# Three score blocks in flight, and the second range's norm ahead of the rotary work, in a two-layer hybrid decoder on one core

## The chip, the core and the metric

The kernel runs on one core of a Trainium2 chip. The core has five engines, each of which takes its own instructions strictly in a fixed order: TensorE (PE, matmuls, with its weight loads listed as PEld), VectorE (DVE), ScalarE (ACT), GpSimd (POOL) and SyncE (SP, which only issues DMAs here). The metric is the device time of one execution in microseconds (us). The kernel before took 1122.07 us, the median of three runs (1121.68 to 1123.77).

## What is computed

A sequence of 16 learned meta tokens and 512 tokens, width 1024, passes two layers. Cut to what matters:

```
a = rmsnorm(h, mix_pre_g);  proj = a @ w_in          # q 512, k 128, v 128, b, c, hc 512 each
q, k = partial_rope(q), partial_rope(k)              # 16 of 64 dimensions are rotated
s = q k^T / 8, causal, window 128, in blocks of 128 queries x 256 keys
m = max(max(s), sink);  e = exp(s - m)
p = e / (sum(e) + exp(sink - m));  y_attn = p @ v
y_conv = b * depthwise_conv3(c * hc)
y = concat(rmsnorm(y_attn), rmsnorm(y_conv)) @ w_out;  h += rmsnorm(y, mix_post_g)
f = relu(rmsnorm(h) @ w_up)^2;  h += rmsnorm(f @ w_down, mlp_post_g)
```

All of it is float32.

## The kernel before

**Tiles.** Activations lie transposed, features on the 128 partitions and tokens along the free dimension, in two token ranges: RA (0 to 272, in layer 1 mostly 16 to 272) and RB (272 to 528). A float32 product is made of two parts for each operand (`a_hi`, `a_lo`, `f_hi`, `f_lo`, `whi`, `wlo`) and three matmuls for each of eight k-steps (`mm3`, traced as L192, L193, L194). A tile of 128 outputs on one range is thus 24 matmuls of 128x256 or 128x272. Weights arrive through SP's queue (L162) and are split by ACT (L107) and DVE (L108).

**Stages.** Each layer runs `first_tiles`, `mixer`, an output projection and a `boundary`; then `first_tiles` again for the MLP's first tiles, `mlp` and a `boundary`. At a boundary `Post` adds the normed result to h for one range: its `start` makes the norm's factor, and `steps(i)` runs two k-steps, each of a multiply (L320 or L322) and an add into h (L323) on DVE, a copy to `a_hi` (L329) and a square (L275) on ACT, the rest `a_lo` (L334) and the sum of squares (L276) on DVE. `first_tiles` runs five tiles on RA (K, V and three of the query tiles q0 to q2, or the MLP's first five) while RB's steps (`pB.steps`) run beside them, then three tiles on RB at once, which need every `a_hi` and `a_lo` of RB, then two more. Tiles leave PSUM through evacuations: for K and queries `rope_evac` copies the raw tile (ACT, L549), sends four small DMAs on SP's queue that swap the rotated halves (L554, L555), and leaves for later the rotary arithmetic (DVE L559 to L561) and the split into parts (K: ACT L598, DVE L603; queries: ACT L610, DVE L613). V is scaled (L577) and later transposed by PE (L583). The MLP's tiles are evacuated at L901.

**The mixer.** A list `plan` holds 26 tiles in order: the last query tile q3 on both ranges, then c, h and b tiles of the convolution. A table filled by `put` says what goes between the tiles of the plan. Attention has eight blocks n, each with three steps: S[n] (`scores`: eight matmuls L198, the masks with the maxima on DVE L655, exponentials on ACT L644, then the sums' reciprocals L647 and L648 and the scaling L650 on DVE), T[n] (`transp`: eight PE transposes L690, whose results are split by ACT L279 and DVE L280 into the tile p), and A[n] (`attend`: four matmuls L198 with V, then L703). Layer 0 has a ninth, small block for the meta tokens (`meta_scores`, `meta_transp` L722, `meta_attend`). S[0] and S[1] are put after plan tiles 4 and 5, T[0] after tile 7, and each further T[n] two or three tiles after the one before (`PERIODS`); S[n+2] stands with A[n]. A score tile S takes a buffer of the ring tagged "w", 14 buffers shared with the split weights and the p tiles; its small companions (`mx`, `ng`, `dn`, `se`) have three buffers each. `fast` keeps two of the MLP's operand sums in a tile `tx` of its own.

**Order.** The program text is not the order of the engines: a scheduler works out at build time, from durations that it assumes, in which order the instructions of each engine stand. On the chip that order is fixed, and each instruction waits for its inputs and for a free buffer.

## Time and profile before

| | before |
|---|---|
| time, median of three runs | 1122.07 us |
| the profiled execution | 1120.94 us, of which its span 1119.2 us and 1.74 us around it |
| PE busy | 1079.4 us, 96% of the span |
| DVE busy | 821.4 us, 73% |
| ACT busy | 627.7 us, 56% |
| mean granted PE clock | 0.987 of full speed |

The span is counted from 0. PE is the engine that does nearly all of the work's time, so the first question at any place is where PE is idle and what ends that idle time. PEclk is the granted clock of PE in shares of full speed. A row of the timeline begins with its start and its busy time in us, and ends with the idle time ahead of it and what released it, if there was any; consecutive equal instructions stand in one row with a count. The busy time of one instruction overlaps that of the next, so that what an instruction costs its engine is the distance from its start to the next one's.

### The profile page before, as it was taken

To read this page: it belongs to the slowest core of one execution; us is meant where nothing else is said; L and a number is where in the kernel's file an instruction comes from. 1 tells how busy PE (TensorE), PEld (TensorE's weight loads), DVE (VectorE), ACT (ScalarE), POOL (GpSimd) and SP (SyncE) were. 2 spreads that over 40 slices of the span, in tenths; PEclk is the share of its full clock that TensorE was granted. 3 is DMA by queue.
4 is the path that set the end of the run, shared out by engine and by line. 5 is a ranking of instruction groups with operands and counts; after the bars stand their busy time and mean duration, and the time that the engine had idled before them with its cause. 6 is when DMAs were issued, how large, how long until landed. Compare 5 with 4: busy or idle time off the path is not lost.

```text
span 1119.2 us, 21378 instructions
## 1 busy us (share of the span) xinstructions
PE 1079.4 (96%) x8066; PEld 1035.5 (93%) x8066; DVE 821.4 (73%) x1943; ACT 627.7 (56%) x1510; POOL 11.2 (1%) x46
## 2 busy tenths in 40 slices
PE   9989899999999999999996999999999999999995
PEld 8989899999999999999986989998889989989995
DVE  7988985978486586486588979869946856856835
ACT  8655656665473274275365556666835724724732
POOL 2000000000000000000000000000000000000000
PEclk9999999999999999999998999999999999999998
DMA  8242221342243243134132322222422522522402
GB/s 249 60 121 77 58 76 57 95 133 71 62 126 102 59 125 110 58 112 143 29 102 60 89 67 62 81 76 76 132 79 73 152 75 76 151 76 76 142 1 76
DMA packets 197608, 102.04 MB, mean 91 GB/s; under 512 B 7360, under 2 KB 197456, under 8 KB 197504
## 3 DMA queue, kind: packets, MB, share of 16 engines
q1 hardware_dynamic: 196640, 99.88, 30.7%
q8 instruction: 63, 1.03, 0.4%
q10 hardware_dynamic: 688, 0.58, 0.2%
q14 instruction: 41, 0.34, 0.1%
q0 software_dynamic: 176, 0.21, 0.1%
HBM read 97.88 MB, written 2.10 MB: 89 GB/s over the span
## 4 chain that ended last, share of the span: by engine, by line
PE 83%; DVE 10%; ACT 2%; DMA 2%; issue 1%; SPq 1%; DVEq 0%; ACTq 0%
PE ps L192 26%; PE ps L194 26%; PE ps L193 26%; PE ps L198 2%; DVE wlo L108 2%; PE ps L690 1%; DMA wraw<-in_w_in 1%; DVE a_lo L334 1%; DVE h L323 1%; DVE acc L276 1%; PE ps L231 1%; DMA h<-in_xT 1%; SPq L554 1%; DMA z<-t 0%; DVE S L655 0%
## 5 line engine op out<-in xcount | busy, mean ns | idle before, releaser
L193 PE MATMUL ps<-f_lo,whi 128*128 128x256 f32 (+2 forms) x1072 | 325.8, 306 | 0.0
L194 PE MATMUL ps<-f_hi,wlo 128*128 128x256 f32 (+2 forms) x1072 | 325.6, 305 | 0.0
L192 PE MATMUL ps<-f_hi,whi 128*128 128x256 f32 (+2 forms) x1072 | 323.0, 307 | 0.0
L192 PE MATMUL ps<-a_hi,whi 128*128 128x256 f32 (+3 forms) x808 | 229.5, 297 | 11.1 <-ACT a_hi L329 9.0
L193 PE MATMUL ps<-a_lo,whi 128*128 128x256 f32 (+3 forms) x808 | 233.6, 293 | 3.7 <-DVE a_lo L334 3.5
L194 PE MATMUL ps<-a_hi,wlo 128*128 128x256 f32 (+3 forms) x808 | 231.7, 291 | 0.0
L194 PEld LDWEIGHTS ps<-f_hi,wlo 128*128 128x128 f32 x1072 | 202.3, 189 | 9.1
L193 PEld LDWEIGHTS ps<-f_lo,whi 128*128 128x128 f32 x1072 | 201.7, 188 | 9.5
L108 DVE TENSOR_TENSOR wlo<-wraw,whi 128x512 fp32r<-128x512 f32 x264 | 173.3, 687 | 49.9 <-ACT whi L107 27.5
L192 PEld LDWEIGHTS ps<-f_hi,whi 128*128 128x128 f32 x1072 | 199.6, 188 | 9.4
L107 ACT ACTIVATE whi<-wraw 128x512 fp32r<-128x512 f32 x264 | 153.6, 623 | 88.6 <-PE ps L193 60.8
L192 PEld LDWEIGHTS ps<-a_hi,whi 128*128 128x128 f32 x808 | 150.1, 192 | 15.7 <-ACT a_hi L329 10.4
L193 PEld LDWEIGHTS ps<-a_lo,whi 128*128 128x128 f32 x808 | 154.8, 192 | 8.5 <-DVE a_lo L334 5.5
L194 PEld LDWEIGHTS ps<-a_hi,wlo 128*128 128x128 f32 x808 | 154.8, 192 | 1.9 <-DVE wlo L108 0.2
L506 DVE TENSOR_TENSOR z<-z,ps 128x272 f32<-128x272 f32 (+2 forms) x78 | 38.0, 487 | 100.2 <-PE ps L194 100.1
L193 PE MATMUL ps<-a_lo,wf 128*128 128x264 f32 (+1 forms) x384 | 108.0, 283 | 0.0
L192 PE MATMUL ps<-a_hi,wf 128*128 128x264 f32 (+1 forms) x384 | 107.9, 283 | 0.0
L194 PE MATMUL ps<-a_hi,wf 128*128 128x264 f32 (+1 forms) x384 | 107.2, 283 | 0.0
L107 ACT ACTIVATE wf<-wraw 128x512 fp32r<-128x512 f32 x96 | 59.7, 626 | 84.2 <-PE ps L193 51.4
L107 ACT ACTIVATE wf<-u 128x512 fp32r<-128x512 f32 x72 | 45.2, 628 | 88.0 <-PE ps L193 73.6
L108 DVE TENSOR_TENSOR wf<-wraw,wf 128x512 fp32r<-128x512 f32 x96 | 65.8, 688 | 11.1 <-ACT wf L107 10.1
L193 PEld LDWEIGHTS ps<-a_lo,wf 128*128 128x128 f32 x384 | 72.3, 188 | 0.1
(175 smaller groups left out, 1813.3 us busy)
## 6 DMA issues: line engine op xcount, KB each, us to landing
wraw<-in_w_up SPq DMA_DIRECT2D x128, 256.0 KB
wraw<-in_w_down SPq DMA_DIRECT2D x128, 256.0 KB
wraw<-in_w_in SPq DMA_DIRECT2D x72, 256.0 KB
wraw<-in_w_out SPq DMA_DIRECT2D x32, 128.0 KB
wraw<-in_w_out SPq DMA_DIRECT2D x16, 256.0 KB
h<-in_xT SPq DMA_DIRECT2D x4, 272.0 KB
h<-in_xT SPq DMA_DIRECT2D x4, 256.0 KB
outT<-h SPq DMA_DIRECT2D x8, 128.0 KB
```

The lines of the kernel that those rows point to most:

```text
L107: ACT.activation(hi, raw, AF.Copy)
L108: DVE.tensor_tensor(lo, raw, hi.bitcast(F32), ALU.subtract)
L192: PE.matmul(ps, whi, ahi, start=first, stop=False, skip_group_check=onto)
L193: PE.matmul(ps, whi, alo, start=False, stop=False, skip_group_check=onto)
L194: PE.matmul(ps, wlo, ahi, start=False, stop=last, skip_group_check=onto)
L198: PE.matmul(ps, a[n], b[n], start=first and n == 0, stop=last and n == 1)
L231: PE.matmul(ps, ones[:, which, :], acc, start=True, stop=more is None)
L276: return (eng or DVE).tensor_tensor(acc, acc, sq, ALU.add)
L323: DVE.tensor_tensor(hk, hk, t, ALU.add)
L334: DVE.scalar_tensor_tensor(a_lo[:, k, t0:t1], hk, g, a_hi[:, k, t0:t1].bitcast(F32), ALU.mult, ALU.subtract)
L506: DVE.tensor_tensor(zz, zz, ps, ALU.add)
L554: nc.sync.dma_start(sw[b:b + 8, :], raw[b + 8:b + 16, :])
```

## The change

Three things are changed.

1. Score tiles get a tag "x" of their own with three buffers. Three blocks of scores are issued ahead (S[0] to S[2] after plan tiles 4, 5 and 6; then S[n+3] with A[n]). T[0] moves from after tile 7 to after tile 8, and every further T[n] stands two tiles after the one before, so that T[7] stands after tile 22 where it stood after 23. `mx`, `ng`, `dn` and `se` have four buffers.
2. The tile `tx` is gone; `mlp` takes three tiles of the tag "x" in its place.
3. In `first_tiles` the next steps of RB's norm are called ahead of the evacuations, two of the four calls after the first group of tiles and two after the next one (`initial`, the kernel's start: one after each of the first four).

```diff
-PERIODS = (2, 2, 3, 2, 2, 3, 2, 2)
+PERIODS = (2, 2, 2, 2, 2, 2, 2, 2)
+AHEAD = 3
...
-    tx = cp.tile([P, 3, 4, L // 2], F32R, name="tx")
...
                 evs += mms([iA[i]], act, hooks)
+            for n in (0, 1)[:1 if initial else 2]:
+                m = next(steps, None)
+                if m is not None:
+                    pB.steps(m)
 
             ready = [evs] if initial else [evs[:3]] if i == at[0] else [[ev] for ev in evs]
...
                 evs = [] if initial else evs[3:] if i == at[0] else []
-            for n in (0, 1)[:1 if len(group) == 1 else 2]:
-                m = next(steps, None)
-                if m is not None:
-                    pB.steps(m)
...
-            S = wp.tile([P, 4, 256], F32, tag="w", name="S", bufs=2 * CAP)
-            mxt = tp.tile([P, 4], F32, tag="mx", name="mx", bufs=3)
+            S = wp.tile([P, 4, L // 2], F32, tag="x", name="S", bufs=3)[:, :, :256]
+            mxt = tp.tile([P, 4], F32, tag="mx", name="mx", bufs=4)
...
-        put(at, S[0])
-        put(at + 1, S[1])
+        for n in range(AHEAD):
+            put(at + n, S[n])
...
-        pos = at + 3
+        pos = at + AHEAD + 1
...
-            if n + 2 < 8:
-                put(pos + 1, S[n + 2])
+            if n + AHEAD < 8:
+                put(pos + 1, S[n + AHEAD])
...
-        tv = [view(k_hi), view(k_lo), view(vv.rearrange("p a b c -> p a (b c)"))] + [tx[:, i, :, :n] for i in range(3)]
+        tv = [view(k_hi), view(k_lo), view(vv.rearrange("p a b c -> p a (b c)"))] + [t[:, :, :n] for t in txs[l]]
...
+        txs[l] = [wp.tile([P, 4, L // 2], F32R, tag="x", name="tx", bufs=3) for _ in range(3)]
```

Line numbers below are those of the kernel before; the changed kernel's lines stand one or two further on from the places of the edits.

What the edits do to the order of an engine shows at three places. The first is DVE at the start of layer 1, while PE runs K, V and the queries: the last steps of RB's norm (L322, L323, L334, L276 in turn) among the rotary work of RA. Before, the last 12 rows up to the second to last `a_lo`:

```order
L559 TENSOR_TENSOR t<-z 128x256
L560 TENSOR_TENSOR t<-t,z 128x256
L322 SCALAR_TENSOR_TENSOR t<-z,gt,s 128x256
L613 TENSOR_TENSOR f_hi<-t,f_hi 64x256
L613 TENSOR_TENSOR f_lo<-t,f_lo 64x256
L561 TENSOR_TENSOR t<-t 128x256
L323 TENSOR_TENSOR h<-h,t 128x256
L560 TENSOR_TENSOR t<-t,z 128x256
L322 SCALAR_TENSOR_TENSOR t<-z,gt,s 128x256
L613 TENSOR_TENSOR f_hi<-t,f_hi 64x256
L613 TENSOR_TENSOR f_lo<-t,f_lo 64x256
L334 SCALAR_TENSOR_TENSOR a_lo<-h,gt,a_hi 128x256
```

And after:

```order
L322 SCALAR_TENSOR_TENSOR t<-z,gt,s 128x256
L334 SCALAR_TENSOR_TENSOR a_lo<-h,gt,a_hi 128x256
L323 TENSOR_TENSOR h<-h,t 128x256
L276 TENSOR_TENSOR acc<-acc,t 128x256
L322 SCALAR_TENSOR_TENSOR t<-z,gt,s 128x256
L334 SCALAR_TENSOR_TENSOR a_lo<-h,gt,a_hi 128x256
L323 TENSOR_TENSOR h<-h,t 128x256
L276 TENSOR_TENSOR acc<-acc,t 128x256
L334 SCALAR_TENSOR_TENSOR a_lo<-h,gt,a_hi 128x256
L276 TENSOR_TENSOR acc<-acc,t 128x256
L108 TENSOR_TENSOR wlo<-wraw,whi 128x512 x5
L559 TENSOR_TENSOR t<-z 128x272
```

K's first rotary row, `L559 t<-z 128x272`, stood ten rows ahead of the first of these, and with it the rotary work of K and of two query tiles stood ahead of or among the last two norm steps; now it stands behind them and behind five weight splits.

The second place is DVE in layer 0's mixer, from the scaling of the second score block (S[1], `L650 128x144 x4`) to that of the meta tokens (`L650 s<-s,dn 64x16 x2`). Before:

```order
L650 TENSOR_SCALAR S<-S,dn 128x144 x4
L647 TENSOR_TENSOR dn<-dn,se 64x2
L648 RECIPROCAL dn<-dn 64x2
L650 TENSOR_SCALAR s<-s,dn 64x16 x2
L280 TENSOR_TENSOR p<-ps,p 128x512 x2
```

And after:

```order
L650 TENSOR_SCALAR S<-S,dn 128x144 x4
L647 TENSOR_TENSOR dn<-dn,se 128x4
L648 RECIPROCAL dn<-dn 128x4
L650 TENSOR_SCALAR S<-S,dn 128x256 x4
L647 TENSOR_TENSOR dn<-dn,se 64x2
L757 TENSOR_TENSOR u<-u,ps 128x256
L765 SCALAR_TENSOR_TENSOR z<-u,gt,z 128x272
L280 TENSOR_TENSOR p<-ps,p 128x512
L648 RECIPROCAL dn<-dn 64x2
L280 TENSOR_TENSOR p<-ps,p 128x512
L765 SCALAR_TENSOR_TENSOR z<-u,gt,z 128x272
L108 TENSOR_TENSOR wlo<-wraw,whi 128x512 x2
```

The meta tokens' scaling, the row after the last of these, moved behind the third score block's scaling, behind both splits of the first block's transposes and behind two weight splits.

The third place is PE around the transposes of the meta tokens (L722). Before, they stand directly ahead of the second score block's transposes (`L690 x8`), behind all of A[0] (`p,vv`):

```order
L198 MATMUL ps<-p,vv 128x512
L193 MATMUL ps<-a_lo,whi 128x256
L194 MATMUL ps<-a_hi,wlo 128x256
L192 MATMUL ps<-a_hi,whi 128x256
L193 MATMUL ps<-a_lo,whi 128x256
L194 MATMUL ps<-a_hi,wlo 128x256
L192 MATMUL ps<-a_hi,whi 128x256
L193 MATMUL ps<-a_lo,whi 128x256
L194 MATMUL ps<-a_hi,wlo 128x256
L722 MATMUL ps<-ident,s 128x64 x2
L690 MATMUL ps<-ident,S 128x128 x8
```

And after, from the rest of the first block's transposes (`L690 x6`) on:

```order
L690 MATMUL ps<-ident,S 128x128 x6
L192 MATMUL ps<-a_hi,whi 128x256
L193 MATMUL ps<-a_lo,whi 128x256
L194 MATMUL ps<-a_hi,wlo 128x256
L192 MATMUL ps<-a_hi,whi 128x256
L193 MATMUL ps<-a_lo,whi 128x256
L194 MATMUL ps<-a_hi,wlo 128x256
L722 MATMUL ps<-ident,s 128x64
L198 MATMUL ps<-p,vv 128x512 x4
```

The first of the two transposes of the meta tokens (L722) now stands six matmuls behind the first block's last transposes, ahead of A[0]; before, both stood behind A[0].

## The prediction

> **What bounds the kernel now.** I read the page first, then the busy time by stage, then the timeline of PE at the stages where it is idle, and last the engines that it waits for there.

> The page says that PE is busy nearly throughout:

> ```profile
> span 1119.2 us, 21378 instructions
> PE 1079.4 (96%) x8066; PEld 1035.5 (93%) x8066; DVE 821.4 (73%) x1943; ACT 627.7 (56%) x1510; POOL 11.2 (1%) x46
> ```

> So PE is idle for 1119.2 - 1079.4 = 39.8 us, and since the change leaves the matmuls as they are, it can win only out of these, and out of slow clock behind them. The stages (PE's busy time is the second number; DVE's the fourth):

> ```profile
> 60.00:80.00 20.00, 15.67 (x117) 15.41 (x116) 16.68 (x67) 10.72 (x35) 0.10 (x1) 0.91 0.39 111
> 130.00:140.00 10.00, 6.66 (x44) 6.48 (x44) 8.90 (x33) 4.03 (x13) 0.00 (x0) 0.84 0.29 83
> 215.00:230.00 15.00, 13.54 (x100) 12.16 (x99) 14.16 (x41) 10.26 (x28) 0.00 (x0) 1.00 0.00 1
> 575.00:600.00 25.00, 14.87 (x103) 13.52 (x103) 21.69 (x56) 12.71 (x33) 0.94 (x3) 0.82 0.14 39
> 640.00:660.00 20.00, 17.36 (x141) 16.69 (x139) 15.49 (x54) 11.33 (x32) 0.10 (x1) 1.00 0.19 54
> 775.00:785.00 10.00, 8.40 (x56) 7.02 (x56) 9.16 (x27) 6.60 (x18) 0.00 (x0) 1.00 0.00 0
> ```

> Idle there: 4.3, 3.3, 1.5, 10.1, 2.6 and 1.6 us, 23.4 in all. The rest lies mostly at the start and at the end, which the change leaves alone. The waits themselves, each in brackets with what ended it:

> ```profile
> 71.41 0.41 PE L690 MATMUL ps<-ident,S 128*128 128x128 f32 x2 [4.33 <-DVE S L650]
> 135.45 0.41 PE L690 MATMUL ps<-ident,S 128*128 128x128 f32 x2 [3.34 <-DVE S L650]
> 597.25 1.01 PE L192 MATMUL ps<-a_hi,whi 128*128 128x256 f32 x3 [7.54 <-ACT a_hi L329]
> 651.53 0.44 PE L690 MATMUL ps<-ident,S 128*128 128x128 f32 x2 [1.28 <-DVE S L650]
> 656.83 0.50 PE L198 MATMUL ps<-p,vv 128*128 128x512 f32 x1 [1.35 <-ACT p L279]
> ```

> The first two and the fourth are transposes that wait for a score block's scaling: T[0] and T[6] of layer 0, and a block of layer 1. The third is the start of RB's tiles in layer 1, waiting for the norm. A long wait costs more than itself. In windows of 1 us the last number but two is the granted clock:

> ```profile
> 72.00:73.00 1.00, 1.00 (x7) 1.00 (x6) 0.93 (x4) 1.00 (x8) 0.07 (x1) 0.50 0.00 0
> 75.00:76.00 1.00, 1.00 (x9) 1.00 (x9) 0.00 (x0) 0.16 (x1) 0.00 (x0) 0.80 0.00 0
> 138.00:139.00 1.00, 1.00 (x6) 1.00 (x6) 0.16 (x1) 0.79 (x4) 0.00 (x0) 0.50 0.06 16
> 652.00:653.00 1.00, 1.00 (x11) 1.00 (x10) 1.00 (x4) 0.00 (x0) 0.00 (x0) 1.00 0.00 0
> ```

> After the waits of 4.33 and 3.34 us PE runs at half clock for some 3.3 us (6 or 7 matmuls a us where the full clock gives 8 to 9), a loss of about 1.6 us each, and the stage of the 7.54 us shows a mean clock of 0.82; after the wait of 1.28 us there is none of it.

> **Layer 0's mixer, the middle and the end.** T[6] stood 3.34 us for its scaling. With three blocks ahead, S[6] is issued one T earlier; counting DVE's instructions in the new order, each at its distance of starts in the trace (a mask 0.34 by the two rows below), its scaling is due at about 113, and PE gets to T[6] at about 129. The wait goes, and so does the half clock: 3.34 + 1.6 = 5.0 us gained. DVE's sum for S[7] is 114 against 137 on PE, so nothing of the kind is late next.

> **Layer 0's mixer, the start.** Here a wait takes the place of the one removed. DVE's rows of before (scaling of S[0], scaling for the meta tokens, the first split):

> ```profile
> 70.97 0.90 DVE L650 TENSOR_SCALAR S<-S,dn 128x144 f32<-128x144 f32 x4
> 74.31 0.37 DVE L650 TENSOR_SCALAR s<-s,dn 64x16 f32<-64x16 f32 x2
> 76.47 1.29 DVE L280 TENSOR_TENSOR p<-ps,p 128x512 fp32r<-128x512 f32 x2 [1.80 <-ACT p L279]
> 80.36 0.42 DVE L655 CUSTOM_DVE_ANT_0 S<-ps,mk 128x256 f32<-128x256 f32 x1
> 80.70 0.42 DVE L655 CUSTOM_DVE_ANT_0 S<-ps,mk 128x256 f32<-128x256 f32 x1
> 81.67 0.34 PE L722 MATMUL ps<-ident,s 64*128 64x64 f32 x2
> ```

> T[0] stands one tile and one score block later on PE (2.95 + 0.95 us of cover), so PE reaches it at 71.0 and not at 67.1. S[2]'s four masks (4 x 0.34) now stand ahead of S[0]'s scaling, which moves from 70.97 to about 72.2. T[0] waits about 1.6 us instead of 4.33, too short for the clock. But the meta tokens' scaling stands behind seventeen more rows, and the way from S[0]'s scaling to it is long: two scalings of 128x144 (2 x 0.82), one of 128x256 (1.05, by size from those), two splits (1.22), two weight splits of the same shape (1.22), four convolution steps of 0.4, two of 0.35 and the small rows between them, 8.6 us in all, so that it ends near 80.8. PE reaches the first L722 behind 24 matmuls and eight transposes, 72.7 + 3.7 = 76.4. It waits 4.4 us, and the matmuls of A[0] queue behind it. By then before and after have done nearly the same (before stood at 80.7 with this work), so T[0]'s gain is all given back, and the new half clock costs what the old one did on top, since the old one is in the 80.7: -1.6 us. This wait is worked out from sums of rows; its bounds are no wait at all (+4.3) and one 1.4 us longer (-3.0).

> **The MLP's boundaries.** RB's norm steps go ahead of the evacuations L901 at the two MLP starts, whose waits are the sums of six short ones:

> ```profile
> PE ps L193 <- DVE a_lo L334: 0.7, 3, 0.3
> PE ps L192 <- ACT a_hi L329: 0.7, 3, 0.2
> 227.27 0.49 DVE L334 SCALAR_TENSOR_TENSOR a_lo<-h,gt,a_hi 128x256 fp32r<-128x256 f32 x1 [0.58 <-ACT a_hi L329]
> ```

> The last `a_lo` came at 227.27; by DVE's sum it now comes at 225.35, while PE without waits wants it at 224.7. Of 1.46 us, 0.65 stays: +0.8 here, as much at 775 to 785, +1.5 together. Bounds: 0, where ACT's copies, not DVE, set the pace (half of the waits name them), and 3.1.

> **The start of layer 1.** The last norm steps stood among the rotary work of RA:

> ```profile
> 587.49 0.44 DVE L559 TENSOR_TENSOR t<-z 128x272 f32<-128x272 f32 x1 [0.86 <-DMA z<-t]
> 598.17 0.42 DVE L323 TENSOR_TENSOR h<-h,t 128x256 f32<-128x256 f32 x1
> 599.17 0.48 DVE L334 SCALAR_TENSOR_TENSOR a_lo<-h,gt,a_hi 128x256 fp32r<-128x256 f32 x1 [0.24 <-ACT a_hi L329]
> 601.41 0.60 PE L231 MATMUL ps<-acc,ones 128*128 128x256 f32 x2
> ```

> In the new order the last add into h is due at 589.7 and the last `a_lo` at 590.2, 9.0 us earlier; PE then runs the three tiles at full clock and ends them at 591.0 instead of 601.41, 10.4 us ahead. The rotary work, though, is not gone, it starts later, and its DMAs with it. SP's first and last of RA's 16 and of RB's 24 rotary DMAs, and the weight loads between them:

> ```profile
> 583.30 0.71 SPq L554 DMA_DIRECT2D z<-t  x1
> 594.02 0.62 SPq L555 DMA_DIRECT2D z<-t  x1
> 602.23 2.81 SPq L162 DMA_DIRECT2D wraw<-in_w_in  x5
> 606.46 0.66 SPq L554 DMA_DIRECT2D z<-t  x1
> 622.18 0.62 SPq L555 DMA_DIRECT2D z<-t  x1
> ```

> They go out every 0.7 us (15.72 / 23 and 10.72 / 15). ACT's raw copies (L549) now stand behind the last `a_hi`, so RA's first goes out at about 590.4 and its last at 601.1; after three weight loads (2.81 / 5 each, 1.7) RB's run from 603.7 to 619.4, 2.8 us earlier than before. On DVE, five weight splits (to 594.9) and all of RA's and RB's rotary work follow. DVE is what limits it then:

> ```profile
> 610.00:640.00 30.00, 29.85 (x250) 29.54 (x248) 28.52 (x92) 16.45 (x48) 1.24 (x5) 1.00 0.31 86
> 624.49 0.42 DVE L613 TENSOR_TENSOR f_hi<-t,f_hi 64x256 fp32r<-64x256 f32 x1
> 626.63 0.28 PE L198 MATMUL ps<-k_hi,f_hi 128*128 128x256 f32 x1
> 626.75 0.28 PE L198 MATMUL ps<-k_lo,f_hi 128*128 128x256 f32 x1
> 633.12 0.41 PE L690 MATMUL ps<-ident,S 128*128 128x128 f32 x2
> ```

> The second half of S[1] needs the query tile q3 of RA, whose split stood at 624.49. DVE's rows up to it add up to 619.75 without a single wait; with some waits for DMAs and ACT, as before, it is 622 to 624. PE, now early, reaches that half at 617.1 after a wait of 1.7 us for V's scaling (L583). It waits 3 to 6.5 us there and loses 1.6 us of clock. With S[2] and one tile more behind it than before's T[0] at 633.12, PE reaches T[0] at 635.9 in the worse case, 1.0 us ahead of before after allowing for that work, and 6.6 us ahead with neither idle DVE nor slow clock. I take 623.0: +2.3 of the 10.4 us. That is nearer the worse end, because all sums without idle time are lower bounds. The bounds below: -1.2 if V's wait too lasts over 3 us.

> **The rest of layer 1's mixer.** Scalings are ready five tiles ahead of their transposes, so the waits of 1.28 and 1.35 go: +2.6 (0 to 3.6, with smaller ones at 630 to 700).

> **Sum.** +5.0 - 1.6 + 1.5 + 2.3 + 2.6 = 9.8 us off the profiled execution's 1120.94, thus 1111.1. That execution ran 1.13 us under the median of 1122.07, so the forecast for the median is 1122.07 - 9.8 = 1112.3. The tile tag for `tx` moves no DVE or PE row; the fourth buffers and S's own ring only lift limits.

> **The clock again.** The 1.6 us behind each new wait are read off the rows: the wait of 3.34 us already dropped it. [...]

> **Rivals.**

> *The whole gain arrives* (chance 0.13). The meta tokens' scaling is not late and q3 arrives as DVE's bare sum says: 4.3 + 5.0 + 3.1 + 6.6 + 3.6 = 22.6, 1099.5 us. For it: DVE has idle time in 74 to 78 (the 1.80 above). Against: DVE is in order, and 8.6 us of rows stand ahead of L722's input.

> *New waits, full clock* (0.10). Two waits of over 4 us that do not drop the clock: 2 x 1.6 more, 1109.1. Against it speak all three waits over 3 us above.

> *Rotary work bounds layer 1's start* (no change, 0.07). If RB's DMAs keep their distance from RA's first (606.46 - 583.30 = 23.2), q3 comes 7.1 us later than before, at 633; PE waits 16 us, and that stage stands 7.8 behind: 5.0 - 1.6 + 1.5 - 7.8 + 2.6 = -0.3, about 1122.4.

> *The table is too dense for DVE* (slower, 0.05). Two periods of three tiles became two in each layer. If DVE's work per block, not the distance from S to T, decides, each of the four places waits a tile, 24 x 0.118 = 2.83 us by the two L198 rows above, 11.3 us in all, and T[6]'s 5.0 do not come: 9.8 - 5.0 - 11.3 = -6.5, 1128.6 us. It decides once DVE runs 16 us later at S[6] than its sum of 113; DVE's idle time, 3.3 of 20 us in the stage from 60 to 80 alone, speaks against that.

> **How the numbers follow.** My case has 0.65. A measurement of this kernel can tell 0.2%, 2.2 us, from no change. Faster by more: 0.65 + 0.13 + 0.10, less 0.02 for my own case's loose end: 0.86. Half of those 0.02 goes to same, with the third rival 0.08, and half to slower, 0.06. The range leaves out the last rival and the outer part of the first: 1103 to 1121.

> **What would show it.** Right: no wait at T[6]; one of about 4 us at L722 with half clock behind it, near 76; RB's tiles in layer 1 start by 584 and end near 591; a wait of 3 to 6 us at the L198 of S[1]. Wrong: waits at transposes in mid mixer, RB's tiles held by a PSUM bank that an evacuation has not freed, or no new wait at all.

## The result, and the profile after

The changed kernel takes 1110.99 us, the median of four runs (1109.8 to 1113.09), against 1122.21 us of the kernel before beside it: a ratio of 0.990, 95% interval 0.988 to 0.992, or 11.2 us. The profiled execution took 1113.09 us with a span of 1111.3 us; it is the slowest of the four, with the lowest mean clock (0.985, the others 0.987 to 0.990). On record stood 1112.3. Two runs took far longer than the others of their kernels and are left out of all medians: one of the kernel before (1758.49 us) and one of the kernel with the meta tokens two tiles later (3321.59 us).

The page of after, against 1119.2 us and 1079.4 us of PE:

```profile
span 1111.3 us, 21393 instructions
PE 1079.6 (97%) x8066; PEld 1038.4 (93%) x8066; DVE 819.8 (74%) x1943; ACT 627.0 (56%) x1510; POOL 11.2 (1%) x46
```

PE's work is the same, its idle time fell from 39.8 to 31.7 us. The stages of after, of which the first, third and last were shown of before:

```profile
60.00:80.00 20.00, 16.27 (x123) 15.87 (x121) 18.45 (x79) 14.58 (x49) 0.10 (x1) 0.91 0.43 123
80.00:100.00 20.00, 17.34 (x113) 16.30 (x114) 14.68 (x52) 7.91 (x26) 0.10 (x1) 0.83 0.19 54
575.00:600.00 25.00, 22.01 (x170) 20.53 (x168) 20.90 (x53) 15.18 (x38) 1.04 (x4) 1.00 0.07 18
600.00:640.00 40.00, 35.21 (x257) 34.97 (x258) 36.76 (x121) 25.38 (x73) 0.20 (x2) 0.87 0.35 98
640.00:660.00 20.00, 20.00 (x161) 19.50 (x160) 18.95 (x67) 12.03 (x34) 0.10 (x1) 1.00 0.28 81
```

PE is idle in places where it was not: 2.7 us in 80 to 100, and 4.8 us in 600 to 640, where it had been idle for 0.15. PE's waits of after between the start and the last stage, in order of time, by the timeline (a wait of 0.96 us at 570.60, which before has too, is left out):

```profile
73.14 0.41 PE L690 MATMUL ps<-ident,S 128*128 128x128 f32 x2 [2.36 <-DVE S L650]
82.66 0.34 PE L722 MATMUL ps<-ident,s 64*128 64x64 f32 x1 [4.03 <-DVE s L650]
225.12 0.39 PE L193 MATMUL ps<-a_lo,whi 128*128 128x256 f32 x1 [0.80 <-DVE a_lo L334]
581.75 0.38 PE L192 MATMUL ps<-a_hi,whi 128*128 128x256 f32 x1 [1.35 <-ACT acc L297]
600.92 0.58 PE L192 MATMUL ps<-a_hi,whi 128*128 128x256 f32 x1 [2.56 <-DVE vv L280]
623.72 0.39 PE L198 MATMUL ps<-k_hi,f_hi 128*128 128x256 f32 x1 [3.87 <-DVE f_hi L613]
775.34 0.39 PE L193 MATMUL ps<-a_lo,whi 128*128 128x256 f32 x1 [0.88 <-DVE a_lo L334]
```

T[6]'s 3.34 us, the 7.54 us at RB's tiles and both waits of 651 and 657 are gone. New are the 4.03 us at the meta tokens' transposes, 2.56 us behind V's transposes and 3.87 us at the second half of S[1]; of the waits for RB's norm in layer 1 the 1.35 us at 581.75 are left.

To see where time went, I take marks on PE that both kernels pass: the L231 matmuls that end each norm. Distances in us, with those of three experiments:

| stretch | before | after | after, again | blocks only | norm only |
|---|---|---|---|---|---|
| start to the end of mixer 0 | 158.83 | 158.32 | 156.75 | 155.78 | 160.96 |
| first MLP start | 15.94 | 13.79 | 13.78 | 15.95 | 13.78 |
| layer 1, start to the end of its mixer | 140.67 | 136.80 | 135.72 | 136.54 | 145.26 |
| second MLP start | 15.89 | 13.81 | 13.80 | 15.90 | 13.80 |

The 7.85 us of this profile are thus 0.5 from the start and mixer 0, 2.15 and 2.1 from the MLP starts and 3.9 from layer 1, less 0.8 in the rest. Most of that 0.8 lies in the two MLPs behind their starts, where PE has no wait in either kernel: between the marks around them after takes 319.63 and 307.53 us, before 319.19 and 307.32. Blocks only has 319.63 too and norm only 319.18, so it comes with the first two edits, one of which moves the tile `tx`; the cause was not looked for.

Layer 1's 3.9 hide a larger movement. RB's three tiles end at:

```profile
588.89 0.59 PE L231 MATMUL ps<-acc,ones 128*128 128x256 f32 x2
```

That is 12.5 us ahead of 601.41, of which 2.3 were brought from the stages earlier (the mark at the start of layer 1 stands at 570.60, before at 572.87) and 10.2 won in this stage. But PE's first T[0] is at 635.37, when before, at 633.12, lacked 3.8 us of work that after has done: only 1.5 us ahead. The 10.2 us of this stage, and 0.7 more, went in between, at the two waits named and at the clock.

### The profile page after: what moved, and what is told of

Read it like the earlier page. It is cut to its first block, busy times and chain, and to the rows that moved or that the text cites. A ratio compares the mean times of both kernels' runs of the same rounds, so it can differ in the third digit from the quotient of the medians.

```text
span 1111.3 us, 21393 instructions
## 1 busy us (share of the span) xinstructions
PE 1079.6 (97%) x8066; PEld 1038.4 (93%) x8066; DVE 819.8 (74%) x1943; ACT 627.0 (56%) x1510; POOL 11.2 (1%) x46
## 4 chain that ended last, share of the span: by engine, by line
PE 83%; DVE 10%; ACT 2%; DMA 2%; issue 2%; SPq 1%; DVEq 0%; ACTq 0%
PE ps L193 26%; PE ps L194 26%; PE ps L192 26%; PE ps L198 2%; PE ps L690 1%; DVE wlo L108 1%; DVE a_lo L334 1%; DVE h L323 1%; DVE acc L276 1%; DMA h<-in_xT 1%; PE ps L231 1%; DMA wraw<-in_w_in 1%; DMA z<-t 0%; ACT whi L107 0%; DVE t L322 0%
## 5 line engine op out<-in xcount | busy, mean ns | idle before, releaser
L193 PE MATMUL ps<-f_lo,whi 128*128 128x256 f32 (+2 forms) x1072 | 326.4, 306 | 0.0
L192 PE MATMUL ps<-f_hi,whi 128*128 128x256 f32 (+2 forms) x1072 | 323.3, 306 | 0.0
L193 PE MATMUL ps<-a_lo,whi 128*128 128x256 f32 (+3 forms) x808 | 232.9, 292 | 1.8 <-DVE a_lo L334 1.7
L192 PE MATMUL ps<-a_hi,whi 128*128 128x256 f32 (+3 forms) x808 | 229.0, 297 | 5.8 <-DVE vv L280 2.6
L108 DVE TENSOR_TENSOR wlo<-wraw,whi 128x512 fp32r<-128x512 f32 x264 | 173.4, 686 | 49.9 <-ACT whi L107 29.0
L193 PEld LDWEIGHTS ps<-f_lo,whi 128*128 128x128 f32 x1072 | 201.4, 188 | 9.4
L192 PEld LDWEIGHTS ps<-f_hi,whi 128*128 128x128 f32 x1072 | 199.9, 188 | 9.3
L193 PEld LDWEIGHTS ps<-a_lo,whi 128*128 128x128 f32 x808 | 155.6, 193 | 5.5 <-DVE a_lo L334 2.6
L192 PEld LDWEIGHTS ps<-a_hi,whi 128*128 128x128 f32 x808 | 151.1, 193 | 9.3 <-DVE vv L280 2.8
L193 PE MATMUL ps<-a_lo,wf 128*128 128x264 f32 (+1 forms) x384 | 108.2, 283 | 0.0
L192 PE MATMUL ps<-a_hi,wf 128*128 128x264 f32 (+1 forms) x384 | 107.9, 283 | 0.0
L108 DVE TENSOR_TENSOR wf<-wraw,wf 128x512 fp32r<-128x512 f32 x96 | 65.6, 687 | 11.3 <-ACT wf L107 10.1
L193 PEld LDWEIGHTS ps<-a_lo,wf 128*128 128x128 f32 x384 | 72.2, 188 | 0.1
```

Source lines behind the costliest of these rows:

```text
L108: DVE.tensor_tensor(lo, raw, hi.bitcast(F32), ALU.subtract)
L192: PE.matmul(ps, whi, ahi, start=first, stop=False, skip_group_check=onto)
L193: PE.matmul(ps, whi, alo, start=False, stop=False, skip_group_check=onto)
```

## The experiments

Each kernel is the changed one but for the edit shown, except where it says otherwise. Times are medians; the kernel before took 1121.6, 1121.5 and 1121.8 us beside the three groups of four, and ratios are to that. A difference to the changed kernel's 1111.0 can be off by 0.4 to 0.7 us, since beside that run the kernel before took 1122.2.

**The norm alone.** The kernel before with the third edit (its diff in the section on the change).

> The kernel before with the third edit alone: RB's norm steps are called ahead of the evacuations, and scores, periods and buffers are those of before. My theory: by the marks on PE the changed kernel gains 3.6 us at the two MLP starts and nothing up to the first transposes of layer 1 (12.5 us ahead at the end of RB's tiles, all given back behind it), so this kernel should gain 3 to 5 us, about 1118. Rival, that the norm's 12.5 us are kept when only two blocks of scores are in flight: about 1106. Second rival, that the edit is worth nothing without the other: 1122.

Measured 1121.1 us, ratio 0.9996 (0.9986 to 1.0007): nothing. In its profile (an execution some 2 us above that median) the MLP starts gain their 2.1 us each, mixer 0 loses 2.1 and layer 1 loses 4.6:

```profile
634.37 0.66 PE L690 MATMUL ps<-ident,S 128*128 128x128 f32 x2 [3.59 <-DVE S L650]
697.90 0.41 PE L690 MATMUL ps<-ident,S 128*128 128x128 f32 x2 [2.43 <-DVE S L650]
```

With only two blocks in flight PE, early, meets transposes whose scaling is late. PE's clock is at half for 30.7 us in the two mixers and at layer 1's start, against 17.1 before. My forecast for this run had counted on no new wait in the mixer and missed by 3 us; the second rival named the outcome.

**The blocks alone.** The changed kernel with the third edit undone, thus the first two edits together; the second was not run alone.

> The changed kernel with the third edit undone: three score blocks, their own buffers and the even periods, the norm's steps behind the evacuations as before. My theory: it keeps what the marks show for the mixers, 0.3 us in layer 0 and 4.6 us in layer 1 from the first transposes on: 4 to 6 us, about 1117. The two parts are then about equal and add up to the whole. Rival, that the even periods are too dense for DVE: waits at transposes in mid mixer and no gain.

1116.0 us, 0.9948 (0.9936 to 0.996), as expected in the sum, but the parts are not equal and do not add up to the whole. Its profile, of the fastest of five executions, has 3.0 us less in mixer 0 and 4.1 in layer 1, where 0.3 and 4.6 were expected, and the wait for the norm much as before:

```profile
594.62 1.01 PE L192 MATMUL ps<-a_hi,whi 128*128 128x256 f32 x3 [6.94 <-ACT a_hi L329]
```

So blocks alone give 5.5 us, the norm alone 0.5, both 11.2: the norm's part pays only with the blocks.

**The changed kernel again.** Nothing edited.

> The changed kernel once more, nothing edited. Every spell of half clock seen so far lasts a whole number of 3.41 us, and within one execution all of them begin on one grid of that step, whose phase differs between executions. My theory: the same waits of 2.4, 4.0, 2.6 and 3.9 us as in its first profile, but other spells behind the two waits under 3 us: each may or may not lower the clock, for 3.4 or 6.8 us, and the executions spread over some 3 us. Rival, that a wait's length alone decides: the same four spells of 3.4, 6.8, 6.8 and 3.4 us again.

1110.6 us (1110.39 to 1110.77), 0.9903 (0.9889 to 0.9917). The executions of this group did not spread by the 3 us expected. But the profile shows waits at the same places, and clock that differs, as expected: V's wait and S[1]'s, on the timeline:

```profile
599.33 0.39 PE L192 MATMUL ps<-a_hi,whi 128*128 128x256 f32 x1 [2.55 <-DVE vv L280]
620.22 0.58 PE L198 MATMUL ps<-k_hi,f_hi 128*128 128x256 f32 x1 [4.68 <-DVE f_hi L613]
```

and a window of 1 us behind the first of them, with the granted clock as the last number but two:

```profile
602.00:603.00 1.00, 1.00 (x10) 1.00 (x9) 1.00 (x4) 0.95 (x4) 0.00 (x0) 1.00 0.16 34
```

V's wait was followed by full clock, where the first profile had 6.8 us at half. From there to S[1]'s second half it is 20.9 us, where it was 22.8, and 0.8 us more of it is waiting. Behind the wait at L722 half clock lasted 3.4 us and not 6.8.

**The meta tokens two tiles later.**

```diff
-            put(at + 5, meta_transp)
-            put(at + 6, meta_attend)
+            put(at + 7, meta_transp)
+            put(at + 8, meta_attend)
```

> The changed kernel with the meta tokens' transposes and attention put two tiles later, the transposes after plan tile 11 and not 9. My theory: the 4.0 us wait at their first transpose is for a scaling that comes late on DVE, and the half clock behind it costs 2.8 us more; both go, 6 to 7 us, about 1104. Rival, that DVE bounds that stage and the wait moves on to the next transposes: under 2 us.

1105.6 us, 0.9858 (0.9844 to 0.9872), some 5 us under the changed kernel, 1 to 2 short of the forecast. The wait is gone, and none of its size took its place; mixer 0 ends at 151.67, against 158.32 and 156.75 in the two profiles of the changed kernel.

**Work for PE in the wait.**

```diff
             S = sbufs.pop("m")
             bk = bank()
+            for _ in range(30):
+                PE.matmul(bk[:, :256], a_hi[:, 0, 0:128], a_hi[:, 1, 0:256], start=True, stop=True)
```

> The changed kernel with 30 matmuls of 128x256 that no one reads in PE's order directly ahead of the meta tokens' transposes, 3.5 us of work in the wait of 4.0 us. They shorten no wait and do no useful work. My theory: with PE busy the clock is not lowered behind it; of the 6.8 us at half clock some 5.6 us carried work, so 2.8 us are gained, about 1108. Rival, that the half clock comes from something other than PE's idle time, or costs nothing: no gain, or 0.5 us lost.

1107.7 us, 0.9876 (0.986 to 0.9892), 3.3 us under the changed kernel though it does 3.5 us more work. The 30 matmuls on the timeline (they carry the line number that the transposes had), and the transposes themselves:

```profile
78.24 3.69 PE L722 MATMUL ps<-a_hi 128*128 128x256 f32 x30
86.25 0.33 PE L724 MATMUL ps<-ident,s 64*128 64x64 f32 x2
```

and the clock behind them:

```profile
83.00:84.00 1.00, 1.00 (x9) 0.92 (x8) 1.00 (x7) 0.00 (x0) 0.00 (x0) 1.00 1.00 295
```

They fill the wait and bring the scaling no sooner: it starts at 82.06, against 82.29 and 81.67 in the two profiles of the changed kernel. But the order changed with them: the transposes themselves now stand behind A[0] and the next scores, at 86.25, without a wait. The stretch from the last matmul ahead of the wait to the second block's first transpose holds the same useful matmuls in all three, and takes 9.0 us here, 12.3 and 11.4 in those two profiles. About 0.7 us of the difference is order, since the 30 matmuls hold PE for 3.5 us where the wait and the transpose behind it held it for 4.3 and 4.2. The rest, 2.6 and 1.7 us, is clock, at 6.8 and 3.4 us of half clock. That PE's idle time costs more than itself is shown by this run, not argued.

**Scores of layer 1 one tile later.**

```diff
-        at = SCORES_AT
+        at = SCORES_AT + (l == 1)
```

> The changed kernel with all score blocks of layer 1 put one plan tile later (S[0] after tile 5). My theory: q3's split on DVE bounds the second half of S[1] at about 623.7; one more tile of 2.85 us in front of it on PE leaves a wait of about 1 us and no half clock behind it: 2.8 us plus 1.7 to 3.4 us of clock, about 1106. Rival, that DVE bounds the whole stage: the wait moves to the first transposes and nothing is gained.

1111.5 us, 0.9914 (0.9901 to 0.9928): no gain, the rival's number. My forecast failed, in its sum and not in its first step. The wait at S[1] fell to 1.69 us and no half clock followed; but five waits came later, four at A[n] (0.56 to 0.84 us, for p) and the longest at the norm of RA's attention rows:

```profile
619.15 0.39 PE L198 MATMUL ps<-k_hi,f_hi 128*128 128x256 f32 x1 [1.69 <-DVE f_hi L613]
677.62 0.67 PE L231 MATMUL ps<-acc,ones 128*128 128x256 f32 x2 [2.15 <-DVE se L641]
```

4.8 us in all. Why DVE and ACT come later there I did not separate from the changed order.

**V's transposes later.**

```diff
-        put(0, mx.v_later[0])
-        put(2, mx.v_later[1])
+        put(2 * (l == 1), mx.v_later[0])
+        put(2 + 2 * (l == 1), mx.v_later[1])
```

> The changed kernel with V's transposes of layer 1 put two plan tiles later, for both ranges. My theory: the 2.6 us wait behind them and its half clock (5 to 6 us in all) go there, but PE then only reaches S[1] earlier, whose data DVE brings no sooner: the wait of 3.9 us there grows, and under 2 us are gained, about 1110. Rival, that V's wait is where the 12.5 us were lost: 5 us or more, 1105.

1113.8 us, 0.9931 (0.9919 to 0.9944): 3 us slower, where a small gain was forecast. As expected V's wait goes (1.04 us for an ACT copy stays) and S[1]'s grows, in fact by more than V's was:

```profile
621.62 0.58 PE L198 MATMUL ps<-k_hi,f_hi 128*128 128x256 f32 x1 [7.54 <-DVE f_hi L613]
```

A wait of 2.70 us at the norm of RA's attention rows (678.84) is new as well.

**All three moved.** Meta tokens two tiles later, and in layer 1 V's transposes and the scores two tiles later.

> The changed kernel with the meta tokens' transposes and attention two plan tiles later, and in layer 1 V's transposes two and all score blocks two plan tiles later. My theory: all three new waits of more than 2.5 us go but a remainder at S[1] of some 4 us less what V's wait had hidden: 5.1 us from the meta tokens, 5 to 9 from layer 1's start, 1098 to 1101. Rival, that DVE is the bound there: no better than 1106, the time with the meta tokens moved alone.

1107.8 us, 0.9873 (0.9859 to 0.9887): no better than the meta tokens moved alone (0.9858), and the rival is right. The waits moved on, the longest to the end of the mixer:

```profile
616.67 0.35 PE L198 MATMUL ps<-k_hi,f_hi 128*128 128x256 f32 x1 [2.94 <-DVE f_hi L613]
633.27 0.50 PE L198 MATMUL ps<-p,vv 128*128 128x512 f32 x1 [2.01 <-ACT p L279]
701.58 1.13 PE L231 MATMUL ps<-acc,ones 128*128 128x256 f32 x4 [3.19 <-DVE acc L276]
```

**No swap DMAs in layer 1.**

```diff
-                for b in (0, 64):
+                for b in (0, 64) if self.l == 0 else ():
```

> The changed kernel without the 40 small DMAs of layer 1 that swap the rotated halves; the rotary arithmetic stays and reads zeros for them, so layer 1's queries and keys are wrong by the swapped parts. This tells SP's queue from DVE as the limit at layer 1's start. My theory, DVE's work limits: the waits of 2.6 and 3.9 to 4.7 us stay within a microsecond, under 2.5 us gained, about 1109. Rival, that SP's issue of a DMA every 0.7 us, or their landing, limits: both waits go, 6 us or more, 1104 or less.

1112.8 us, 0.992 (0.9906 to 0.9934): no gain. The waits did not stay as I expected: V's shrank to 0.52 us, a wait of 2.69 us came at the norm of RA's attention rows (678.28), and the one at S[1] is longer:

```profile
620.69 0.55 PE L198 MATMUL ps<-k_hi,f_hi 128*128 128x256 f32 x1 [6.39 <-DVE f_hi L613]
```

From the end of RB's tiles to that matmul, DVE's busy time (the fourth number) in the changed kernel's first profile and here:

```profile
588.89:623.72 34.83, 28.41 (x214) 27.92 (x212) 30.17 (x86) 20.02 (x54) 0.20 (x2) 0.90 0.23 62
588.22:620.69 32.47, 25.56 (x214) 25.16 (x212) 31.74 (x87) 21.47 (x51) 0.20 (x2) 0.98 0.39 114
```

Without the DMAs DVE is idle for 0.7 us of the 32.5, so its work is the bound here. In the changed kernel it is idle for 4.7 us; one wait for a swap DMA has 1.82 of them. The run is not a clean removal, since the order changed with it: 14 weight splits (L108) stand ahead of q3's split, where the changed kernel has 8, 3.7 us of DVE work more. So SP's queue, to which the prediction gave a paragraph, is not what bounds this stage; what it costs through DVE's 1.8 us of waiting is not settled.

**No rotary arithmetic on DVE in layer 1.**

```diff
-                    DVE.tensor_tensor(u, sw, st[:, t0:t1], ALU.mult)
-                    DVE.tensor_tensor(raw, raw, ct[:, t0:t1], ALU.mult)
-                    DVE.tensor_tensor(raw, raw, u, ALU.add)
+                    if self.l == 0:
+                        DVE.tensor_tensor(u, sw, st[:, t0:t1], ALU.mult)
+                        DVE.tensor_tensor(raw, raw, ct[:, t0:t1], ALU.mult)
+                        DVE.tensor_tensor(raw, raw, u, ALU.add)
```

> The changed kernel without the three DVE instructions of each rotary evacuation in layer 1 (30 instructions, 10 us of DVE work); the swap DMAs stay, the result is not used, so layer 1's queries and keys are not rotated. My theory, DVE's work limits layer 1's start: the wait at S[1] and that behind V's transposes go with their half clock, 6 to 10 us, 1101 to 1105. Rival, that PE or the score blocks limit there: under 2 us.

1100.3 us, 0.9811 (0.9798 to 0.9823): 10.7 us under the changed kernel. Where after's PE was busy for 35.21 of 40 us, it is now

```profile
600.00:640.00 40.00, 39.72 (x331) 39.23 (x330) 33.05 (x117) 24.84 (x75) 0.30 (x3) 1.00 0.40 111
```

and both waits are gone. Nothing waits for the swap DMAs here either, and fewer weight splits (5 and not 8) stand ahead of q3's split; but the run before this, with no DMAs at all, kept the wait. Together they show that DVE's work in front of q3's split is what took the 10 us of this stage back.

**The norm ahead at the MLP starts only.** In layer 1 the steps stand behind the evacuations as before.

```diff
+            ahead = initial or norm == "z"
-            for n in (0, 1)[:1 if initial else 2]:
+            for n in (0, 1)[:(1 if initial else 2) if ahead else 0]:
...
+            for n in (0, 1)[:0 if ahead else 1 if len(group) == 1 else 2]:
+                m = next(steps, None)
+                if m is not None:
+                    pB.steps(m)
```

> The changed kernel with the norm's steps ahead of the evacuations at the kernel's start and at the two MLP starts, but behind them, as before, at the start of layer 1. My theory, from the marks: layer 1's start gains nothing from the edit (from the end of layer 0 to the end of layer 1's mixer it is 136.5 us without it and 135 to 137 with it), so this is as fast as the changed kernel, 1110 to 1112. Rival, that layer 1's 12.5 us are kept in part: 1113 or more.

1114.2 us, 0.9935 (0.9922 to 0.9948), some 3 us behind the changed kernel: the rival's number, so layer 1 keeps a part of the edit's gain. By the marks layer 1 takes 138.80 us here.

**The same with the meta tokens later.**

> The kernel of the run before this with the meta tokens' transposes and attention two plan tiles later as well. My theory: the two edits add up, about 5 us under that run, 1105 to 1107, as fast as the changed kernel with the meta tokens moved alone. Rival, that they overlap: 1109.

1106.8 us, 0.9868 (0.9853 to 0.9882), within the forecast, though 7.4 us under the run before this and not 5. Layer 1 takes 137.07 us. Without the edit in layer 1 it is 136.5, 137.1 and 138.8 us in three kernels, with it 134.8 to 136.8 in four (after twice, the meta tokens moved, the filled wait), 1.6 us less on average, though the two groups overlap. By the medians the edit in layer 1 is worth 3.2 us without the meta tokens moved (1114.2 against 1111.0) and 1.1 with them (1106.8 against 1105.6). So of this stage's 10 us 1 to 3 are kept.

The lowest median is that of the changed kernel with the meta tokens moved, 1105.6 us.

## Why the prediction was right, point by point

*Mixer 0, T[6]:* right. No wait stands there, and no half clock.

*Mixer 0, the start:* the new wait is there, 4.03 us against 4.4 forecast, at 82.66 and not 80.8. The step's clock was mis-sized. I had T[0]'s wait at 1.6 us, "too short for the clock"; it is 2.36 us, and the clock fell (3.4 us at half, a loss of 1.7). I had 1.6 us for the clock at L722; it was 6.8 us at half, of which 5.6 carried work, a loss of 2.8. These 2.9 us turn the forecast's +3.4 for mixer 0 into the 0.5 of this profile. In the second profile, with half as much half clock behind L722, mixer 0 gains 2.1. The run with PE's wait filled puts 2.6 and 1.7 us on the clock behind L722 in the two profiles; the one with the meta tokens moved gains some 5 us with the wait.

*MLP starts:* +1.5 forecast with a bound of 3.1, +4.2 measured, the term most mis-sized. The remaining wait, 0.80 us, is as worked out (0.65). What I took too small is what the six waits of before cost, by their idle time of 1.46. The rows show why, in before, a k-step without a wait and one with 0.20 us:

```profile
217.94 0.52 PE L192 MATMUL ps<-a_hi,whi 128*128 128x256 f32 x3
218.30 0.28 PE L193 MATMUL ps<-a_lo,whi 128*128 128x256 f32 x1
218.42 0.28 PE L194 MATMUL ps<-a_hi,wlo 128*128 128x256 f32 x1
221.16 0.51 PE L192 MATMUL ps<-a_hi,whi 128*128 128x256 f32 x3
221.87 0.39 PE L193 MATMUL ps<-a_lo,whi 128*128 128x256 f32 x1 [0.20 <-DVE a_lo L334]
222.09 0.28 PE L194 MATMUL ps<-a_hi,wlo 128*128 128x256 f32 x1
```

From the first row to the third it is 0.48 us, from the fourth to the sixth 0.93: the wait cost 0.45 us, not 0.20. A matmul's busy time (0.28) overlaps the next one's by 0.16 us, and the idle time counts only from its end; the first matmul behind a wait takes 0.10 longer. Six such waits cost 3.0 us, the one of after 1.05, and 1.95 of the 2.1 us are found.

*Layer 1's start:* too high. RB's tiles ended at 588.89 where I said 591.0; 2.3 us came from the stages before, so the stage's first step, 10.2 us against 10.4, was as worked out. The waits at V (2.56 against 1.7) and at S[1] (3.87, within 3 to 6.5) are there, but V's took 6.8 us of half clock with it that I had not priced, and S[1]'s data came at 623.7, 2 us later than my 622 to 624 when those 2.3 us are taken off:

```profile
609.68 0.43 DVE L749 TENSOR_TENSOR u<-ps,z 128x258 f32<-128x258 f32 x1 [1.55 <-PE ps L194]
623.24 0.42 DVE L613 TENSOR_TENSOR f_hi<-t,f_hi 64x256 fp32r<-64x256 f32 x1
```

The first of these rows has most of the 2 us: behind V's wait and its half clock, DVE in turn waited 1.55 us for a tile of PE. In the second profile, without that half clock, this row has no wait, and from the end of RB's tiles to the split it takes 32.4 us and not 34.4.

Up to T[0] the stage gave -0.7 us in the first profile and +0.3 in the second (where T[0] starts at 632.71), against +2.3. The bound that I named, DVE's work, is shown by the two runs that leave work or DMAs out.

*The rest of layer 1's mixer:* too low. +2.6 forecast, 4.6 in both profiles. Before listed 3.6 us of waits there (1.28, 1.35 and 0.95) and after 0.3. If each cost 0.25 us more than its idle time, as at the MLP starts, that makes about 3.8; where the rest comes from is open.

*Rivals:* "new waits, full clock" fails, since the clock fell behind all four waits in the first profile; in the second it stayed up behind one, V's. "Too dense for DVE": no wait stands at any score block's transposes behind T[0]. "Rotary work bounds layer 1's start" put the bound on the DMAs' distance; without the DMAs nothing is gained. I had the new tile for `tx` moving no row of PE; with the first two edits PE takes 0.6 us longer in the two MLPs, by which of them is open.

The places of the large waits and what ends them were right, but that the sum came out so near is luck, because its errors were of both signs: about 2.9 us too much in mixer 0 and 2 to 3 at layer 1's start, 2.7 too little at the MLP starts and 2 in the rest of layer 1. The forecast of 9.8 lies between the 7.85 us of the profiled execution and the 11.2 of the median.

## What to carry to other kernels

Follow a wait that is removed to the next thing that PE needs: here 10 us won at one place were worth 1 to 3, because an engine with a fixed order had the same work to do before the next matmul, while waits of 0.2 us in a series cost twice what their idle times say (0.45 us for 0.20). Two edits that are worth 0.5 and 5.5 us apart were worth 11.2 together, so parts of a change are measured both alone and undone. Where a wait cannot be removed, fill it or move the waiting step behind other work: for the 4.03 us at the meta tokens' transposes both paid, 3.3 us and some 5 us, and the clock behind the filled wait stayed at 1.00.

## What the runs showed of the hardware

```profile
74.00:75.00 1.00, 1.00 (x10) 1.00 (x9) 0.96 (x6) 1.00 (x6) 0.03 (x1) 0.81 0.00 0
81.00:82.00 1.00, 0.00 (x0) 0.00 (x0) 1.00 (x3) 0.00 (x0) 0.00 (x0) 0.72 0.00 0
600.00:601.00 1.00, 0.08 (x1) 0.08 (x1) 0.97 (x3) 0.98 (x4) 0.00 (x0) 0.64 0.13 36
624.00:625.00 1.00, 1.00 (x7) 1.00 (x7) 0.94 (x5) 0.83 (x3) 0.00 (x0) 0.58 0.77 201
```

The starts are 74.62, 81.44, 600.28 and 624.16; the distances, 6.82, 518.84 and 23.88 us, are 2.00, 152.0 and 7.00 times 3.413 us. The spells last 3.4, 6.8, 6.8 and 3.4 us (half clock in the first 15 us and behind the last matmuls is not counted, here and below). In the profile of before, windows of 1 us give starts at 71.98, 136.84 and 590.80 and lengths of 3.4, 3.4 and 10.2 us; the distances, 64.86 and 453.96 us, are 19.00 and 133.0 times 3.413 us. The phase is another one there: 71.98 lies 2.64 us ahead of 74.62. What sets the step and the phase is not shown.

PE's idle time can be counted in stretches of that step. In after, the stretches directly ahead of the four spells hold 1.93, 2.82, 1.91 and 2.97 us of the waits at T[0], L722, V and S[1]; in before, those ahead of the three spells hold 2.84 and 2.03 us of a single wait and 2.32 us of two. In these two profiles the longest idle time in a stretch with full clock in it and behind it is 1.49 us (before, 65.16 to 68.57). With V's transposes later, 1.70 us of a single wait (612.37 to 615.78) had full clock behind them; but two waits in one stretch had half clock behind them at 1.81 us together with the norm ahead at the MLP starts only (582.25 to 585.66), and at 1.55 with the meta tokens moved as well (578.21 to 581.62, where the second is the start of a wait of 7.54). Whether there is a limit between 1.70 and 1.91 us of a single wait, and what besides idle time counts, is not shown. In after, 1.21 us idle in 81.44 to 84.86 were followed by another 3.4 us of half clock, and so were 0.65 us in the stretch from 600.28; every spell of these two profiles ends behind a stretch without a listed wait.

A wait's length alone did not decide: behind V's wait of 2.56 us the first profile of the changed kernel has 6.8 us of half clock, and behind the one of 2.55 us the second has full clock. I take the place of a wait on the grid for the reason, also for the reason why the first four executions of the changed kernel lay between 1109.8 and 1113.1 us, with mean clocks from 0.990 to 0.985 in that order; this is an estimate and not shown, since only one execution of each group has a trace, and the four of the second group lay within 0.4 us. Differences of 2 us between such kernels need several executions.
